# A hybrid decoder layer on Trainium2: three feature tiles of the GLU's input loaded and split during k, y reloaded in place of summed, DMA scratch set to 512 bytes

## The chip, the cores and the metric

The kernel runs on one core of one Trainium2 chip. The metric is the device time of one execution in microseconds (us); before the change it is 688.62 us, the median of 3 runs (688.46 to 688.71).

## The reference, cut to what matters

One layer: RMS norm, one wide projection, windowed attention beside a state space block with a GLU (gated linear unit), an output projection, and a gate from an embedding. 1024 tokens, width 1024, 8 heads of 64.

```python
z = rms_norm(h, mix_norm) @ w_in
q, k, v, gate_a, u, gate_s = jnp.split(z, splits, axis=-1)
attn = dilated_mixture_attention(q, k, v, q_norm, k_norm) * jax.nn.silu(gate_a)
...
yg = jax.nn.gelu(y, approximate=False)                    # y: the S5 scan's output, 512 features
ssm = yg * jax.nn.sigmoid(yg @ w_glu + b_glu) * jax.nn.silu(gate_s)
h = h + jnp.concatenate([attn, ssm], axis=-1) @ w_out
gate = jax.nn.sigmoid(rms_norm(h, ple_norm) @ w_ple_gate)
h = h + gate * (p @ w_ple_proj)
```

## The kernel before

Every float32 product is made of three fp32r matmuls (`mm3`, lines 106 to 109): each operand is split into a high part (a copy by ScalarE, ACT) and a low part (source minus high part, by VectorE, DVE, or GpSimd, POOL). Activations lie feature major, 128 features on the partitions and 512 tokens in a tile.

The stages follow each other: the u projection and the S5 scan (its gelu output goes to DRAM as `yg_s`, 4 feature tiles of 128 by 2 halves of 512 tokens); the gates (to `sg_s`, `sa_s`); q, then k, token major (lines 694 to 731); v (863 to 873); the GLU (877 to 921); the output projection of the state space half (`os`, 953), which is woven with attention; that of the attention half (`oa`, 974); the embedding gate. Attention is a generator (line 754): `step(n)` lets it advance by n heads. It makes scores into PSUM tiles `sc`, masks them and takes the row minimum on DVE (line 780, `p`), the exponential on ACT (803), splits them into two f16 halves `hl` (806 to 810), transposes these by a DMA into `pt` (812) and multiplies them with v into `pv` (818).

No order is written out by hand: the Tile framework places the instructions of each engine by a priority (`tc.high_priority`) and its own model of time, and each engine then runs its list in that order. Every DMA of this kernel is issued by SyncE (the queue SP), also the transposes `pt`; SP waits in order too.

The GLU before. Each of the 8 tiles `yl` (4 features by 2 token halves) is loaded into one of the four buffers `ev` (lines 897 to 899) and split into `ygh`, `ygl` (900), which lie in the pool `mp`. This pool is opened after `ph1.close()` (line 875), in the room of the x tiles that the v projection reads until its end. For each of 8 output tiles (n, f), 12 matmuls make `glu` in PSUM. Then:

```python
E[RY].tensor_tensor(y, yg[n][0][:, f].bitcast(F32), yg[n][1][:, f].bitcast(F32), op=OP.add)   # 915
nc.sync.dma_start(gl, sg_s[f * P:(f + 1) * P, c])                                              # 916
E[EG[f]].tensor_tensor(y, y, gl, op=OP.mult)                                                   # 917
A.activation(gl, o, AF.Tanh, bias=bg[:, f:f + 1], scale=0.5)                                   # 918
stt(y, gl, 1.0, y, OP.add, OP.mult)                                                            # 919
split(ms_[n][0][:, f], ms_[n][1][:, f], y, E[EM[f]])                                           # 920
```

Here `RY` is "V", so line 915 builds y again on DVE as the sum of its two parts; line 917 is on POOL, 918 on ACT, 919 and the split's low part on DVE. `y` (tile `ym`) and `gl` (tile `gm`) take two of the four `ev` buffers. In the trace line 919 appears as L281 and the splits as L736 (ACT) and L737 (DVE or POOL).

## Time and profile before

| | |
|---|---|
| median of 3 runs | 688.62 us (688.46 to 688.71) |
| the profiled execution: span from first to last instruction | 686.2 us |
| what lies around the span, taken from the median | 2.4 us |
| PE busy | 630.0 us, 92% |
| DVE busy | 496.8 us, 72% |
| POOL busy | 302.0 us, 44% |
| ACT busy | 289.5 us, 42% |
| bytes moved by DMA | 87.25 MB, mean 127 GB/s |

No time of its own is listed for the profiled execution; 688.6 us (its span and the 2.4 us around it) stands for it. PE is TensorE's matmuls, DVE VectorE, ACT ScalarE, POOL GpSimd. Busy shares over the whole span hide the stages: one has to ask for the busy time of each engine in a stretch, for what ended PE's idle time there, and for the clock that TensorE was granted. A DMA share is the mean busy share of 16 DMA engines, and can pass 1 where packets overlap.

### The profile page before, as it was taken

To read this page: it belongs to the slowest core of one execution; us is meant where nothing else is said; L and a number is where in the kernel's file an instruction comes from. 1 tells how busy PE (TensorE), PEld (TensorE's weight loads), DVE (VectorE), ACT (ScalarE), POOL (GpSimd) and SP (SyncE) were. 2 spreads that over 40 slices of the span, in tenths; PEclk is the share of its full clock that TensorE was granted. 3 is DMA by queue.
4 is the path that set the end of the run, shared out by engine and by line. 5 is a ranking of instruction groups with operands and counts; after the bars stand their busy time and mean duration, and the time that the engine had idled before them with its cause. 6 is when DMAs were issued, how large, how long until landed. Compare 5 with 4: busy or idle time off the path is not lost.

```text
span 686.2 us, 10942 instructions
## 1 busy us (share of the span) xinstructions
PE 630.0 (92%) x3836; PEld 491.9 (72%) x3836; DVE 496.8 (72%) x1126; ACT 289.5 (42%) x553; POOL 302.0 (44%) x230
## 2 busy tenths in 40 slices
PE   9997799777879999999899789889999999999997
PEld 6875577566768788877677556566677888888786
DVE  6999999899998557767553998957944766626322
ACT  7532123445576624348434646534513455113100
POOL 3433825866775224234332845422432437342641
PEclk9999899998999999999999889989999999999999
DMA  7803612323444746754661868899987243015101
GB/s 257 241 7 109 209 38 76 105 79 93 77 92 92 167 69 125 159 86 125 161 122 48 216 147 148 213 192 191 217 226 244 94 152 124 15 63 165 50 32 61
DMA packets 158119, 87.25 MB, mean 127 GB/s; under 512 B 117232, under 2 KB 130416, under 8 KB 158064
## 3 DMA queue, kind: packets, MB, share of 16 engines
q1 hardware_dynamic: 158064, 86.56, 50.7%
q8 instruction: 30, 0.49, 0.3%
q14 instruction: 25, 0.20, 0.1%
HBM read 48.81 MB, written 17.27 MB: 96 GB/s over the span
## 4 chain that ended last, share of the span: by engine, by line
PE 46%; DVE 26%; DMA 12%; issue 7%; ACT 5%; POOL 2%; SPq 1%; DVEq 0%; ACTq 0%; POOLq 0%
PE gt L108 4%; PE gt L109 4%; PE gt L107 3%; DMA wr<-in_w_in 3%; DMA pt<-hl 3%; PE oa L107 2%; PE oa L109 2%; PE oa L108 2%; DVE tmp L270 2%; PE q L109 2%; PE q L107 2%; PE q L108 2%; DVE wl L158 2%; DVE p L780 2%; PE k L108 2%
## 5 line engine op out<-in xcount | busy, mean ns | idle before, releaser
L158 POOL TENSOR_TENSOR wl<-wr,wh 128x512 fp32r<-128x512 f32 x34 | 49.4, 1457 | 67.8 <-ACT wh L157 44.5
L157 ACT ACTIVATE wh<-wr 128x512 fp32r<-128x512 f32 x68 | 41.9, 626 | 51.4 <-DMA wr<-in_w_in 22.4
L810 POOL TENSOR_TENSOR hl<-p,hl 128x384 f16<-128x384 f32 (+2 forms) x34 | 38.9, 1148 | 53.9 <-ACT hl L807 27.1
L107 PE MATMUL g<-xh,wh 128*128 128x512 f32 x128 | 52.6, 411 | 7.3 <-DVE gate L640 5.5
L109 PE MATMUL g<-xh,wl 128*128 128x512 f32 x128 | 52.5, 410 | 5.3 <-DVE wl L158 5.3
L803 ACT ACTIVATE p<-p,st 128x384 f32<-128x384 f32 (+4 forms) x64 | 39.8, 622 | 39.1 <-DVE st L780 38.9
L108 PE MATMUL g<-xl,wh 128*128 128x512 f32 x128 | 52.0, 407 | 0.0
L108 PE MATMUL gt<-hl,wh 128*128 128x512 f32 (+1 forms) x136 | 51.7, 381 | 0.0
L107 PE MATMUL gt<-hh,wh 128*128 128x512 f32 (+1 forms) x136 | 51.7, 382 | 0.0
L109 PE MATMUL gt<-hh,wl 128*128 128x512 f32 (+1 forms) x136 | 51.2, 382 | 0.0
L158 DVE TENSOR_TENSOR wl<-wr,wh 128x512 fp32r<-128x512 f32 x34 | 34.8, 1025 | 19.1 <-ACT wh L157 14.0
L1016 ACT ACTIVATE gg<-gg 128x512 f32<-128x512 f32 (+1 forms) x17 | 10.1, 605 | 67.4 <-DVE gg L270 67.2
L1018 POOL TENSOR_TENSOR gg<-gg,hs 128x512 f32<-128x512 f32 x14 | 18.0, 1290 | 43.1 <-DVE gg L270 41.5
L107 PEld LDWEIGHTS g<-xh,wh 128*128 128x128 f32 x128 | 24.6, 192 | 13.7 <-DVE gate L640 6.5
L270 DVE TENSOR_TENSOR gg<-gt,rrow 128x512 f32<-128x512 f32 (+1 forms) x17 | 10.8, 656 | 32.7 <-PE gt L109 32.6
L109 PEld LDWEIGHTS g<-xh,wl 128*128 128x128 f32 x128 | 24.7, 193 | 12.0 <-DVE wl L158 6.6
L818 PE MATMUL pv<-vv,pt 128*128 128x64 f16 x504 | 24.4, 198 | 6.3 <-DMA pt<-hl 6.2
L818 PEld LDWEIGHTS <-pt 128*128 128x128 f16 x504 | 19.0, 101 | 14.8 <-DMA pt<-hl 8.9
L107 PEld LDWEIGHTS gt<-hh,wh 128*128 128x128 f32 x136 | 25.6, 188 | 5.5
L108 PEld LDWEIGHTS gt<-hl,wh 128*128 128x128 f32 x136 | 25.6, 188 | 5.4
L109 PEld LDWEIGHTS gt<-hh,wl 128*128 128x128 f32 x136 | 25.6, 188 | 5.4
L780 DVE CUSTOM_DVE_ANT_0 p<-sc,mask,gc 128x128 f32<-128x128 f32 (+3 forms) x56 | 24.3, 458 | 6.7 <-PE sc L793 3.2
(330 smaller groups left out, 1957.2 us busy)
## 6 DMA issues: line engine op xcount, KB each, us to landing
wr<-in_w_in SPq DMA_DIRECT2D x48, 256.0 KB, 2.9
xr<-in_x SPq DMA_DIRECT2D x16, 256.0 KB, 4.7
wr<-in_w_out SPq DMA_DIRECT2D x16, 256.0 KB, 3.3
xos<-in_x SPq DMA_DIRECT2D x16, 256.0 KB, 4.0
h_s<-xos SPq DMA_DIRECT2D x16, 256.0 KB, 3.4
xoa<-h_s SPq DMA_DIRECT2D x16, 256.0 KB, 2.8
wr<-in_w_ple_gate SPq DMA_DIRECT2D x16, 256.0 KB, 3.0
out_t<-gg SPq DMA_DIRECT2D x15, 256.0 KB, 2.0
```

The lines of the kernel that those rows point to most:

```text
L107: T.matmul(o, lh, rh, start=first, stop=False)
L108: T.matmul(o, lh, rl, start=False, stop=False)
L109: T.matmul(o, ll, rh, start=False, stop=last)
L157: A.activation(hi, raw, AF.Copy)
L158: E[lo_on[k % len(lo_on)]].tensor_tensor(lo, raw, hi.bitcast(F32), op=OP.subtract)
L270: V.tensor_tensor(o, x, y, op=op)
L780: V.tensor_tensor_reduce(out, sc, msk, gm, init, op0=OP.add, op1=OP.min, accum_out=acc_[:, hd:hd + 1])
L803: A.activation(pb_, pb_, AF.Exp, bias=mx[:, hc], scale=-1.0, accum_out=dn[:, hc])
L810: E[LE[b][h0 % len(LE[b])]].tensor_tensor(hl[:, na:2 * na], pr_[:, 0:na], hl[:, 0:na], op=OP.subtract)
L818: T.matmul(pv[:, hd], pt[:, nf + i * nt + j + na * lp, :], vv[:, k0 + j, hd, lv, :], start=first, stop=end and not nf and j == n - 1 and l ...
L1016: A.activation(gt_, gt_, AF.Sigmoid)
L1018: (V if last else Q).tensor_tensor(gt_, gt_, hs, op=OP.add)
```

## The change

Four edits. (1) `RY` becomes "D": y of the GLU's gate is read again from `yg_s` by a DMA, in place of the sum on DVE. (2) Of token half 0, feature tiles 0, 1 and 2 are loaded and split inside the k loop, ahead of the row pairs 0, 1, 2, into two tiles of a new pool `y0p` that lies in room of its own. (3) In the GLU stage feature tile 3 of half 0 gets two tiles `yx` in `mp`; the two four-tile buffers `ygh0`, `ygl0` of `mp` are no longer taken. (4) `dynamic_dma_scratch_size` is set to 512 bytes per partition; the built program before reserves 16384 there. Comments are also cut.

```diff
-RY = "V"
+RY = "D"
...
+    y0p = ph2.enter_context(tc.tile_pool(name="y0p", bufs=1))
...
+    y0 = tuple(y0p.tile([P, 3, 512], F32R, name=f"yg{x}0") for x in "hl")
     for which, c0 in (("q", 0), ("k", 512)):
         w = [load_w(wp, a["w_in"], k, c0) for k in range(KT)]
         for bp in range(4):
+            if which == "k" and bp < 3:
+                y = ev(f"yl{bp}0")
+                nc.sync.dma_start(y, yg_s[bp * P:(bp + 1) * P, 0:512])
+                split(y0[0][:, bp], y0[1][:, bp], y, E[EY[bp]])
...
     for n in range(2):
-        yg.append((quad(f"ygh{n}"), quad(f"ygl{n}")))
+        if n:
+            yh_, yl_ = quad(f"ygh{n}"), quad(f"ygl{n}")
+            yg.append(tuple([t_[:, k] for k in range(4)] for t_ in (yh_, yl_)))
+        else:
+            yg.append(tuple([t_[:, k] for k in range(3)] + [mp.tile([P, 512], F32R, tag="yx", name=f"yx{j}", bufs=2)]
+                            for j, t_ in enumerate(y0)))
         for k in range(4):
+            if not n and k < 3:
+                continue
             y = ld(f"yl{k}{n}")
...
-    nc = bacc.Bacc("TRN2", target_bir_lowering=False, num_devices=1)
+    nc = bacc.Bacc("TRN2", target_bir_lowering=False, num_devices=1, dynamic_dma_scratch_size=512)
```

`EY = "QVQVQVQV"` puts the low parts of the tiles k = 0 and 2 of half 0 on POOL (Q) and that of k = 1 on DVE (V).

The framework places everything anew. Three places of its lists follow; names end in a running number that differs between the two programs, and lines of the change stand 6 to 13 higher from the k loop on (`split` is L697 in the change, L737 before; the mask's row minimum is L786, was L780).

**SP during k.** Here `qh`, `ql`, `ks` are the transposed q and k, `wr` the raw weights of v. Before:

```order
L725 DMA_TRANSPOSE qh_2296<-qh5_2631 128x8x128
L152 DMA wr2_1024_3138<-in_w_in 128x512
L726 DMA_TRANSPOSE ql_2297<-ql5_2632 128x8x128
L725 DMA_TRANSPOSE qh_2296<-qh6_2715 128x8x128
L726 DMA_TRANSPOSE ql_2297<-ql6_2716 128x8x128
L725 DMA_TRANSPOSE qh_2296<-qh7_2722 128x8x128
L726 DMA_TRANSPOSE ql_2297<-ql7_2723 128x8x128
L731 DMA_TRANSPOSE ks_2298<-k0_2854 128x8x128
L731 DMA_TRANSPOSE ks_2298<-k1_2859 128x8x128
```

With the change:

```order
L735 DMA_TRANSPOSE qh_2299<-qh5_2636 128x8x128
L152 DMA wr2_1024_3155<-in_w_in 128x512
L705 DMA yl00_2781<-yg_s_67 128x512
L736 DMA_TRANSPOSE ql_2300<-ql5_2637 128x8x128
L735 DMA_TRANSPOSE qh_2299<-qh6_2720 128x8x128
L736 DMA_TRANSPOSE ql_2300<-ql6_2721 128x8x128
L705 DMA yl10_2872<-yg_s_67 128x512
L735 DMA_TRANSPOSE qh_2299<-qh7_2727 128x8x128
L736 DMA_TRANSPOSE ql_2300<-ql7_2728 128x8x128
L741 DMA_TRANSPOSE ks_2301<-k0_2863 128x8x128
L705 DMA yl20_2963<-yg_s_67 128x512
L741 DMA_TRANSPOSE ks_2301<-k1_2868 128x8x128
```

The three loads stand between transposes that the k stage issues anyway.

**DVE at the start of the GLU.** `sc31` is block 3's scores of head 1, `p` their masked copy, `hl` its f16 halves. Before:

```order
L737 TENSOR_TENSOR ygl0_3712<-yl10_3717,ygh0_3711 128x512
L737 TENSOR_TENSOR ygl0_3712<-yl30_3725,ygh0_3711 128x512
L809 CAST hl26_3947<-p26_3941 128x384
L281 SCALAR_TENSOR_TENSOR vv_3124<-v7_3618,vscale_3125,vv_3124 128x8x64
L780 ISA p31_4190,st3_4148<-sc31_4191,mask_2313,gc_2305 128x512
L780 ISA st3_4148 128x1
L158 TENSOR_TENSOR wl3_0_3708<-wr3_0_3705,wh3_0_3707 128x512
L809 CAST hl23_3819<-p23_3813 128x384
L809 CAST hl24_3861<-p24_3855 128x384
L270 TENSOR_TENSOR ga0_4112<-at0_4114,ga0_4112 128x512
L737 TENSOR_TENSOR ygl1_3730<-yl11_3735,ygh1_3729 128x512
L915 TENSOR_TENSOR ym00_3762<-ygh0_3711,ygl0_3712 128x512
```

With the change:

```order
L697 TENSOR_TENSOR yx1_3729<-yl30_3730,yx0_3728 128x512
L697 TENSOR_TENSOR ygl1_3735<-yl11_3740,ygh1_3734 128x512
L815 CAST hl26_3952<-p26_3946 128x384
L786 ISA p31_4195,st3_4153<-sc31_4196,mask_2316,gc_2308 128x512
L786 ISA st3_4153 128x1
L281 SCALAR_TENSOR_TENSOR vv_3141<-v7_3635,vscale_3142,vv_3141 128x8x64
L270 TENSOR_TENSOR ga0_4117<-at0_4119,ga0_4117 128x512
L158 TENSOR_TENSOR wl3_0_3725<-wr3_0_3722,wh3_0_3724 128x512
L815 CAST hl23_3824<-p23_3818 128x384
L815 CAST hl24_3866<-p24_3860 128x384
L786 ISA p32_4218,st3_4153<-sc32_4219,mask_2316,gc_2308 128x512
L786 ISA st3_4153 128x1
```

The low part of tile 1 and the sum `ym00` are gone from this piece, half 1's first low part has moved up by nine places, and the next scores follow.

**SP in the middle of the GLU.** `pt` is an attention transpose, `gm` the gate load, `ym` the reload of y. Before:

```order
L812 DMA_TRANSPOSE pt30_4159<-hl30_4156 128x8x128
L916 DMA gm20_3847<-sg_s_65 128x512
L812 DMA_TRANSPOSE pt27_4101<-hl27_4098 128x6x128
L812 DMA_TRANSPOSE pt31_4199<-hl31_4196 128x8x128
L152 DMA wr4_512_4051<-in_w_out 128x512
L152 DMA wr5_512_4057<-in_w_out 128x512
L916 DMA gm30_3889<-sg_s_65 128x512
L812 DMA_TRANSPOSE pt32_4222<-hl32_4219 128x8x128
```

With the change:

```order
L926 DMA ym20_3851<-yg_s_67 128x512
L152 DMA wr4_512_4056<-in_w_out 128x512
L818 DMA_TRANSPOSE pt30_4164<-hl30_4161 128x8x128
L818 DMA_TRANSPOSE pt31_4204<-hl31_4201 128x8x128
L929 DMA gm20_3852<-sg_s_65 128x512
L818 DMA_TRANSPOSE pt32_4227<-hl32_4224 128x8x128
L926 DMA ym30_3893<-yg_s_67 128x512
L152 DMA wr5_512_4062<-in_w_out 128x512
L818 DMA_TRANSPOSE pt33_4267<-hl33_4264 128x8x128
L929 DMA gm30_3894<-sg_s_65 128x512
```

Each tile now has two loads that wait for an `ev` buffer, where it had one, and attention's transposes stand behind both.

## Rows read from the trace of the kernel before

**Rows 1.** The page: span, and busy time of each engine over it.

```profile
span 686.2 us, 10942 instructions
PE 630.0 (92%) x3836; PEld 491.9 (72%) x3836; DVE 496.8 (72%) x1126; ACT 289.5 (42%) x553; POOL 302.0 (44%) x230
```

**Rows 2.** Busy time by stretch: k, v's end, the GLU and a piece of it, attention.

```profile
core 0: us, PE busy (x) PEld busy (x) DVE busy (x) ACT busy (x) POOL busy (x), PEclk, DMA share, GB/s
280.00:300.00 20.00, 20.00 (x87) 16.10 (x86) 12.63 (x43) 7.28 (x12) 4.09 (x4) 1.00 0.69 117
360.00:370.00 10.00, 10.00 (x53) 7.96 (x49) 1.45 (x4) 2.62 (x5) 0.00 (x0) 1.00 0.01 2
374.20:445.00 70.80, 58.82 (x585) 40.52 (x586) 68.87 (x141) 41.72 (x91) 42.67 (x33) 0.88 0.77 176
...
400.00:410.00 10.00, 7.34 (x49) 5.03 (x49) 10.00 (x17) 4.78 (x11) 4.41 (x4) 0.66 0.71 165
445.00:521.00 76.00, 71.51 (x883) 50.95 (x871) 50.99 (x133) 28.95 (x62) 24.11 (x19) 0.96 0.98 210
```

**Rows 3.** PE's groups in 374.2 to 445: busy, mean ns, idle before, releasers.

```profile
L793 PE MATMUL sc<-ks,qh 128*128 128x256 f16 (+1 forms) x21 | 6.9, 344 | 4.3 <-DVE st L780 4.3
...
L750 PE MATMUL sc<-ks,qh 128*32 128x128 f16 x60 | 3.1, 228 | 4.0 <-DVE st L780 3.9
...
L818 PE MATMUL pv<-vv,pt 128*128 128x64 f16 x198 | 9.7, 203 | 1.8 <-DMA pt<-hl 1.8
```

**Rows 4.** DVE's group of the sum in 374.2 to 445, columns as in rows 3.

```profile
L915 DVE TENSOR_TENSOR ym<-ygh,ygl 128x512 f32<-128x512 f32 x8 | 10.0, 1248 | 0.0
```

**Rows 5.** Tiles ym and yl: duration ns minimum, median, maximum; first and last start.

```profile
L915 DVE TENSOR_TENSOR ym<-ygh,ygl x8: 678/1240/1782, 383.4 to 426.9; 128x512 f32<-128x512 f32 x8
...
L899 SPq DMA_DIRECT2D yl<-yg_s x8: 319/327/572, 326.6 to 378.5; - x8
L736 ACT ACTIVATE ygh<-yl x8: 613/631/638, 373.0 to 382.8; 128x512 fp32r<-128x512 f32 x8
L737 POOL TENSOR_TENSOR ygl<-yl,ygh x4: 1290/1293/1712, 373.7 to 384.2; 128x512 fp32r<-128x512 f32 x4
L737 DVE TENSOR_TENSOR ygl<-yl,ygh x4: 826/1262/1778, 375.5 to 385.3; 128x512 fp32r<-128x512 f32 x4
...
DMA to landing us min/median/max: 2.6/3.6/4.6
```

**Rows 6.** Timeline of PE: first and last matmul of two GLU tiles (start, us).

```profile
403.73 0.79 PE L107 MATMUL glu<-ygh,wh 128*128 128x512 f32 x1 [0.80 <-ACT gm L918]
...
408.58 0.63 PE L109 MATMUL glu<-ygh,wl 128*128 128x512 f32 x1
...
411.25 0.47 PE L107 MATMUL glu<-ygh,wh 128*128 128x512 f32 x1
...
413.89 0.40 PE L109 MATMUL glu<-ygh,wl 128*128 128x512 f32 x1
```

**Rows 7.** SP's waits in 374 to 460 at gate loads: us, times, longest.

```profile
SPq L916 <- DVE msl L737: 2.5, 2, 1.3
...
SPq L916 <- DVE ym L281: 1.9, 1, 1.9
...
SPq L916 <- DVE ygl L737: 1.4, 1, 1.4
...
SPq L916 <- DVE hl L809: 1.0, 1, 1.0
SPq L916 <- DVE st L780: 0.9, 1, 0.9
```

**Rows 8.** The page: DMA queues, packets, MB, share of 16 engines.

```profile
q1 hardware_dynamic: 158064, 86.56, 50.7%
q8 instruction: 30, 0.49, 0.3%
q14 instruction: 25, 0.20, 0.1%
```

More of the change, by code (lines that the diff above doesn't have):

```diff
@@ L692, in per_head, with split @@
         return x.unsqueeze(2).to_broadcast([P, 8, 64])
+    def split(hi, lo, src, eng=Q):
+        A.activation(hi, src, AF.Copy)
+        eng.tensor_tensor(lo, src, hi.bitcast(F32), op=OP.subtract)
+    y0 = tuple(y0p.tile([P, 3, 512], F32R, name=f"yg{x}0") for x in "hl")
     for which, c0 in (("q", 0), ("k", 512)):
@@ L733, in hybrid_layer @@
     ma, ms_ = {}, {}
-    def split(hi, lo, src, eng=Q):
-        A.activation(hi, src, AF.Copy)
-        eng.tensor_tensor(lo, src, hi.bitcast(F32), op=OP.subtract)
     def mdense(b, n):
@@ L899, in hybrid_layer @@
                 nc.sync.dma_start(y, yg_s[k * P:(k + 1) * P, n * 512:(n + 1) * 512])
-                split(yg[n][0][:, k], yg[n][1][:, k], y, E[EY[4 * n + k]])
+                split(yg[n][0][k], yg[n][1][k], y, E[EY[4 * n + k]])
     for n in range(2):
@@ L906, in hybrid_layer @@
             for k in range(4):
-                mm3(o, w[k][0][:, f * P:(f + 1) * P], w[k][1][:, f * P:(f + 1) * P], yg[n][0][:, k], yg[n][1][:, k],
+                mm3(o, w[k][0][:, f * P:(f + 1) * P], w[k][1][:, f * P:(f + 1) * P], yg[n][0][k], yg[n][1][k],
                     k == 0, k == 3)
@@ L914, in hybrid_layer @@
                 else:
-                    E[RY].tensor_tensor(y, yg[n][0][:, f].bitcast(F32), yg[n][1][:, f].bitcast(F32), op=OP.add)
+                    E[RY].tensor_tensor(y, yg[n][0][f].bitcast(F32), yg[n][1][f].bitcast(F32), op=OP.add)
                 nc.sync.dma_start(gl, sg_s[f * P:(f + 1) * P, c])
```

## The prediction

> **What bounds the kernel now.** I read the page's busy shares first: PE is busy 630.0 of 686.2 us [rows 1]. So at most 56 us of idle time are there to be won, and one must know in which stage they lie. Busy time by stretch is the second view [rows 2]. During k PE has no gap (20.00 of 20 us) and the others have room. At the end of v, from 360 to 370, DVE does 1.45 us of work in 10 and POOL none. Then, from 374.2 to 445, the roles turn: DVE is busy 68.87 of 70.8 us and PE only 58.82, at a mean granted clock of 0.88. This is the GLU stage, woven with attention, and it is the one that the change touches. From 445 to 521 PE is busy 71.51 of 76 and DVE 50.99: PE leads again.
>
> The third view is what ended PE's idle time in the GLU stage [rows 3]. The scores wait 4.3 and 3.9 us for the mask's row minimum on DVE (L780), pv only 1.8 us for a transpose. So DVE is what is waited for, not because L780 is long but because it queues in a full DVE. Of PE's 12.0 us idle (70.8 less 58.82) 8.2 are put down to DVE.
>
> The fourth is PE's timeline [rows 6]. After pauses the granted clock falls: it is 0.66 between 400 and 410 [rows 2], part of that stretch at 1.2 GHz and part at 2.4. A GLU tile of 12 matmuls took 5.48 us there (403.73 to 409.21), and 3.04 us from 411.25 on, at 2.4 GHz. A stall of PE thus costs more than its own length.
>
> **The sums that go from DVE.** Line 915 runs 8 times, 9.99 us in all (8 times 1248 ns [rows 4]). One DVE split of half 0, tile 1, leaves this stage too: 1.26 us at its median there [rows 5]. Together 11.25 us, the upper end. The same instructions in their shortest form took 678 and 826 ns [rows 5], which makes 6.25 us, the lower end: the sum's range of 678 to 1782 ns for one and the same shape says that more than the arithmetic is in it, and POOL is busy 42.67 of these 70.8 us [rows 2]. If the excess is waiting for POOL, another instruction may inherit it. I take the middle, 8.8 us, since POOL loses only two of its 33 instructions here, and most conflicts stay with the remaining splits.
>
> The Trainium skill says this outright (SBUF — State Buffer, section Who interferes with whom): a DVE instruction with two SBUF inputs contends with a GpSimd instruction that reads SBUF, and a DMA contends with no engine. By that rule the excess is time in a lock that passes to another instruction, the relief would be only the lower end, and the kernel would take 685.0 us; by the row alone it would be 680.0. The trace agrees as far as the spread of the durations goes; who inherits the wait no run here shows.
>
> Is a shorter DVE list worth its full length? DVE is full from 400 to 410 and nearly so over the stage [rows 2], and PE has 12 us of idle time to give back, more than the relief, so up to there neither PE nor the later part caps it; I pass it on one to one. The stretch from 445 on has PE busy 94%, so an earlier start moves it as a whole.
>
> **The loads that come.** Eight reloads `ym` are issued by SP at 327 ns each, by the row of `yl`, the same 256 KB of the same tensor [rows 5]: 2.6 us. SP works in order, and the lists show attention's transposes directly behind them. I charge all 2.6 us to the path; if SP has slack it is 0, the lower end. The `ym` load stands one to three transposes ahead of its `gm` load, so it lands before that, and line 917, which waits for both, is held no longer than by `gm`. As for bandwidth, 8 times 256 KB are 2.1 MB; the stage moves 176 GB/s at a share of 0.77 [rows 2], about 229 GB/s at full share, so the reloads add 9.2 us of all engines' time and lift the share to about 0.90. I take nothing for it, as the stretch behind runs at 0.98 with PE busy 94%; at most the 1.8 us that pv waits for transposes double.
>
> **The splits that move to k.** Three loads (1.0 us of SP), three ACT copies (1.9 us at 631 ns), two POOL subtractions (2.6 us at 1293 ns) and one on DVE (1.26 us at the median) [rows 5] now stand in k. Cover: between 280 and 300 ACT is busy 7.28 of 20 us, POOL 4.09, DVE 12.63, with PE never idle [rows 2]. I take 0. If the cover fails, it is because the three tiles take turns in the four `ev` buffers with the raw k tiles and hold up their evacuation; then ACT and DVE parts add up to 3.2 us.
>
> **What the early splits bring at the GLU's start.** Before, the first `ygh` copy starts at 373.0, as v ends, since its tile lies in v's room, and the last low part at 385.3 [rows 5]. Now tiles 0 to 2 are there, tile 3 and half 1 follow at once, so the elementwise chain starts some us earlier. This is no term of its own: while DVE is full, what starts earlier only fills DVE earlier.
>
> **The scratch.** All data moves on one queue of kind hardware_dynamic, and there are two for instructions [rows 8]; no queue of another kind is in the trace that would use the reserved room. Costs nothing; it makes room for the new tiles.
>
> **Sum.** Against the profiled execution (686.2 us and 2.4 around it, equal to the median by how I took it): 688.6 - 8.8 + 2.6 = **682.4 us**, 0.9% less. Its own ends: 688.6 - 11.25 = 677.4 with nothing paid on SP, and 688.6 - 6.25 + 2.6 + 1.8 = 686.8; 677.4 to 686.8 is this case's own range.
>
> **The rivals.**
>
> 1. *Deeper: DVE's relief also keeps the clock up.* All 11.25 us go, SP pays nothing, and the slow GLU tile between 403 and 409 runs as the next one did (5.48 - 3.04 = 2.4 us): 688.6 - 11.25 - 2.4 = 675.0 us. For it: the clock is under 1 in the very stretches where PE waits for DVE. Against: SP's new loads, and PE will still pause.
>
> 2. *Slower: SP's queue takes DVE's place.* A `ym` load cannot go out before its `ev` buffer is free, and SP holds everything behind it, transposes above all. Gate loads wait in just this way today: 2.5 us in two, 1.9, 1.4, 1.0 and 0.9 in one each [rows 7], a mean of 1.28 us over six. If each of the eight reloads stalls SP by that and its 327 ns, and attention feels it in full, 12.9 us come in and 8.8 go: 692.7 us. It decides from 8.8 / 8 = 1.1 us per reload, issue and stall, on. For it: both loads of a tile now wait for buffers which DVE and POOL free late. Against: six of the eight gate loads already wait so, and the second load of a tile finds a buffer of the same pair; a freer DVE frees buffers sooner; and transposes have some lead (pv lost 1.8 us in the stage). The Trainium skill (DMA: Bandwidth & Descriptors, section Anatomy of one DMA) states the rule behind this case: DMA engines wait for no semaphore, the issuing sequencer does so ahead of dispatch. The rows of SP's waits agree.
>
> 3. *Nothing: the stage is held by latency, not by DVE's load.* With four `ev` buffers only two output tiles are in flight; each goes through loads (2.6 to 4.6 us to land), POOL, ACT, DVE, ACT, DVE. If this loop sets the pace, DVE gets idle and the end stays: 688.6 us. For it: the loop has the same number of buffers as before. Against: the DVE is full now, so the loop isn't what waits.
>
> That the change doesn't do what it says can be set aside: the lists show neither L915 nor half 0's old splits in the GLU.
>
> **Chances.** About 0.2% (1.4 us) is what a measurement of this kernel can tell from no change. The forecast case gets 0.53, rival 1 0.13, rival 2 0.22, rival 3 0.12. Faster by over 0.2%: the first two, 0.66. Within 0.2%: 0.12. Slower by over 0.2%: 0.22. The predicted time is the forecast's, 682.4. The range starts at 676.0, leaving out the deep half of rival 1, and ends at 691.0, past the middle of rival 2 (1.4 us per reload, stall and issue, against 1.6 for its full price); outside lie some 0.06 and 0.10.
>
> **What would show it.** In the changed profile, DVE's busy time falls by 5 to 11 us over the span, with no line for the sum. If the forecast holds, the GLU stage shrinks by some 6 us, PE's waits for L780 (8.2 us) shrink by about half and the k stage keeps PE at 20 in 20. If rival 2 holds, SP's waits at the `ym` loads stand in the queue's view with over 1 us each, and pv's wait for `pt` rises well over 1.8 us. If rival 3 holds, DVE shows idle time before the tanh or line 917 while the stage keeps its length. If rival 1 holds, the granted clock between 380 and 440 is at 1.0 in most slices. I would be wrong altogether if the k stage gained PE gaps over 3 us, or if the framework's new order of attention left PE without work behind 445, where I counted on a plain shift.

## The result, and the profile after

The changed kernel takes **693.56 us** (median of 4 runs, 692.91 to 695.77) against 688.66 us for the kernel before on the same chip: ratio 1.0075, 95% interval 1.0051 to 1.0100. It is slower by 4.9 us, where 682.4 was forecast, and 2.6 us above the end of the range. (Run 2 below holds one execution of 847.46 us and run 5 one of 701.48 us that count as slow; the ratios leave them out, the medians do not.)

The profiled execution took 692.91 us, 691.1 of them in its span. The page, answering to [rows 1]:

```profile
span 691.1 us, 10937 instructions
...
PE 632.7 (92%) x3836; PEld 494.8 (72%) x3836; DVE 489.7 (71%) x1118; ACT 289.1 (42%) x553; POOL 304.8 (44%) x230
```

DVE does 7.1 us less than before, as intended. Where the time went is read stage by stage, from the first and last matmul of each kind of tile in the trace:

| stage | before | after | difference |
|---|---|---|---|
| start to first q matmul (same lists on every engine) | 222.1 | 224.3 | +2.2 |
| q, and k until the first v matmul | 95.0 | 95.4 | +0.4 |
| first v to first GLU matmul ("v stage") | 57.1 | 60.5 | +3.4 |
| first GLU to last `os` matmul ("GLU stretch", attention woven in) | 146.0 | 139.7 | -6.3 |
| last `os` to first `oa` matmul ("gap") | 0.3 | 1.9 | +1.6 |
| first to last `oa` matmul | 50.7 | 53.8 | +3.1 |
| embedding gate, to the last `gt` matmul | 109.9 | 110.4 | +0.5 |

In this execution the gain stands just where it was forecast, and in its size (a second execution, run 5, shows 4.3 us of it); it is lost ahead of it and behind it. Busy time by stretch, each stretch moved by 6 us (k by 2) against those of [rows 2]:

```profile
core 0: us, PE busy (x) PEld busy (x) DVE busy (x) ACT busy (x) POOL busy (x), PEclk, DMA share, GB/s
282.00:302.00 20.00, 20.00 (x87) 16.10 (x86) 10.18 (x34) 6.63 (x11) 5.33 (x5) 1.00 0.56 118
...
380.20:451.00 70.80, 60.36 (x666) 41.82 (x665) 65.51 (x155) 45.02 (x102) 43.26 (x33) 0.90 0.98 210
...
451.00:527.00 76.00, 70.49 (x805) 51.34 (x804) 47.10 (x111) 24.66 (x50) 24.59 (x17) 1.00 0.91 206
```

In the GLU stage DVE has room again (65.51 of 70.8 us, it was 68.87), PE is busier, and the DMA engines go from a share of 0.77 to 0.98. PE's groups there, answering to [rows 3]:

```profile
L824 PE MATMUL pv<-vv,pt 128*128 128x64 f16 x216 | 10.1, 196 | 7.7 <-DMA pt<-hl 7.6
L799 PE MATMUL sc<-ks,qh 128*128 128x256 f16 (+2 forms) x25 | 8.0, 342 | 2.1 <-DVE st L786 2.1
...
L756 PE MATMUL sc<-ks,qh 128*32 128x128 f16 x68 | 3.9, 226 | 0.2 <-DVE st L786 0.2
```

The waits for the row minimum on DVE fell from 8.2 to 2.3 us; the waits for transposes rose from 1.8 to 7.6. What DVE gave, the transposes took back in part. The reloads alone do not explain that: from 374 to 525 PE waits 5.6 us for transposes before, 11.0 with the change, and also 10.6 with the early splits alone (run 3) and 7.8 with neither sum nor reload (run 11).

**Ahead of it: k's side chain.** PE has no gap in k, but the work beside it falls behind. ScalarE's timeline in k: start, us, engine, line, operation, and in brackets the idle time before it with what ended it:

```profile
279.51 1.06 ACT L733 ACTIVATE qh<-rawq 128x1024 f16<-128x1024 f32 x1 [0.46 <-DMA qh<-qh]
286.02 0.63 ACT L696 ACTIVATE ygh<-yl 128x512 fp32r<-128x512 f32 x1 [5.45 <-DMA yl<-yg_s]
286.56 0.58 ACT L714 ACTIVATE sqk<-k 128x512 f32<-128x512 f32 x1
...
296.81 0.63 ACT L696 ACTIVATE ygh<-yl 128x512 fp32r<-128x512 f32 x1 [2.32 <-DMA yl<-yg_s]
...
306.98 0.63 ACT L696 ACTIVATE ygh<-yl 128x512 fp32r<-128x512 f32 x1 [3.18 <-DMA yl<-yg_s]
```

ScalarE runs its list in order; it stands three times, 10.9 us in all, before the copy of an early tile that has not landed, with the evacuation of k (`sqk`, L714, and `rawk`, L718) behind it. Not all of this is new idle time: before, ScalarE stood there 5.9 us for a raw q tile from POOL and 4.8 until a transpose had landed, and from 268 to 318 its busy time only falls from 25.4 to 22.9 us. What counts is that the work on k comes later. The casts of k, last start in the row, end that chain. Before and after, by tile:

```profile
L729 ACT ACTIVATE k<-rawk x8: 614/631/632, 294.7 to 327.7; 128x512 f16<-128x512 f32 x8
```

```profile
L739 ACT ACTIVATE k<-rawk x8: 614/629/652, 300.7 to 333.9; 128x512 f16<-128x512 f32 x8
```

The last one starts 10.6 us behind the first v matmul (317.1) before, 14.2 behind it (319.7) after. v's evacuations and attention's first heads are in the same lists, and PE pays in v: it waits longer for `vv` on DVE. PE's waits from 314 to 382, before and after (us, times, longest):

```profile
PE v L107 <- DVE vv L281: 1.3, 1, 1.3
```

```profile
PE v L107 <- DVE vv L281: 2.9, 1, 2.9
```

The v stage has the same 324 matmuls in both. PE's idle time in it goes from 2.9 to 4.5 us and its busy time from 54.2 to 56.0, at a mean granted clock of 0.97 for 1.00: the clock fell behind this wait (last section). With the early splits alone (run 3) the clock stays at 1.00, and the idle time is 5.5 us.

**Behind it: the last weights of `oa`.** The half of `w_out` that `oa` needs is loaded second (the runs' texts call it the second half), through two raw tiles, and its four last tiles can be cast only when the last `os` matmuls have read the tiles in their place. SyncE's and then ScalarE's, DVE's and PE's timelines after, around the last `os` matmul (519.92):

```profile
515.84 0.39 SPq L766 DMA_DIRECT2D ga<-sa_s  x1
...
517.84 0.46 SPq L964 DMA_DIRECT2D h_s<-xos  x1
520.96 2.25 SPq L948 DMA_DIRECT2D xoa<-h_s  x2
523.31 0.38 SPq L964 DMA_DIRECT2D h_s<-xos  x1
524.88 0.81 SPq L152 DMA_DIRECT2D wr<-in_w_out  x2
```

```profile
521.11 0.63 ACT L696 ACTIVATE mah<-ga 128x512 fp32r<-128x512 f32 x1 [5.67 <-DVE ga L270]
521.68 1.28 ACT L157 ACTIVATE wh<-wr 128x512 fp32r<-128x512 f32 x2
529.63 1.30 ACT L157 ACTIVATE wh<-wr 128x512 fp32r<-128x512 f32 x2 [6.67 <-DMA wr<-in_w_out]
```

```profile
530.96 1.19 DVE L158 TENSOR_TENSOR wl<-wr,wh 128x512 fp32r<-128x512 f32 x1 [5.40 <-ACT wh L157]
...
532.68 0.68 DVE L281 SCALAR_TENSOR_TENSOR xoa<-oa,xoa 128x512 f32<-128x512 f32 x1
```

```profile
530.03 0.40 PE L109 MATMUL oa<-mah,wl 128*128 128x512 f32 x1
533.41 0.51 PE L107 MATMUL oa<-mah,wh 128*128 128x512 f32 x1 [2.99 <-DVE xoa L281]
```

Read backwards: PE stands 2.99 us because both PSUM tiles of `oa` are full; the one due is emptied by DVE, in whose list the weights' low part stands first; that waits for ScalarE's cast, the cast for a load, and the load went out at 524.88, behind loads of `xoa` and spills on SyncE. SyncE's own waits from 490 to 535, before and after:

```profile
SPq L935 <- DMA h_s<-xos: 10.2, 7, 2.5
```

```profile
SPq L948 <- DMA h_s<-xos: 18.2, 8, 5.1
```

A buffer of `ev` comes free when the spill from it has landed, and until then the next load into it holds SyncE's whole list. Attention now ends at 503.4 instead of 509.7, so more `os` tiles follow each other through these buffers undiluted; that this is why SyncE waits longer is not shown. Run 3 speaks against it as the whole reason: there attention ends at 519.9, SyncE's waits for spills are 10.6 us, much as before the change, and `oa` loses more. What the losing kernels share is when the last two weights' loads go out. SyncE's timeline before and in run 3, where the last `os` matmul starts at 520.22 and 522.64:

```profile
520.76 0.85 SPq L152 DMA_DIRECT2D wr<-in_w_out  x2
```

```profile
527.86 2.23 SPq L152 DMA_DIRECT2D wr<-in_w_out  x2
```

They go out 0.5 us behind the last `os` matmul before, 5.0 us behind it with the change and 5.2 us in run 3.

### The profile page after: what moved, and what is told of

It is laid out like the page before. It is cut to its first block, busy times and chain, and to the rows that moved or that the text cites. A ratio compares the mean times of both kernels' runs of the same rounds, so it can differ in the third digit from the quotient of the medians.

```text
span 691.1 us, 10937 instructions
## 1 busy us (share of the span) xinstructions
PE 632.7 (92%) x3836; PEld 494.8 (72%) x3836; DVE 489.7 (71%) x1118; ACT 289.1 (42%) x553; POOL 304.8 (44%) x230
## 4 chain that ended last, share of the span: by engine, by line
PE 38%; DVE 24%; DMA 16%; issue 8%; ACT 6%; POOL 5%; SPq 2%; POOLq 0%; ACTq 0%; DVEq 0%
DMA pt<-hl 4%; DMA wr<-in_w_in 4%; PE gt L108 4%; PE gt L109 4%; PE gt L107 4%; DVE tmp L270 2%; PE oa L107 2%; PE oa L108 2%; PE oa L109 2%; DVE wl L158 2%; DVE y L578 2%; DVE tmp L275 1%; DVE p L786 1%; PE g L108 1%; POOL wl L158 1%
## 5 line engine op out<-in xcount | busy, mean ns | idle before, releaser
L158 POOL TENSOR_TENSOR wl<-wr,wh 128x512 fp32r<-128x512 f32 x34 | 50.9, 1500 | 62.8 <-ACT wh L157 60.2
L816 POOL TENSOR_TENSOR hl<-p,hl 128x384 f16<-128x384 f32 (+2 forms) x34 | 41.9, 1232 | 59.0 <-ACT hl L813 31.8
L157 ACT ACTIVATE wh<-wr 128x512 fp32r<-128x512 f32 x68 | 41.9, 626 | 46.0 <-DMA wr<-in_w_in 25.4
L107 PE MATMUL g<-xh,wh 128*128 128x512 f32 x128 | 54.3, 424 | 5.4 <-DVE gate L640 5.4
L109 PE MATMUL g<-xh,wl 128*128 128x512 f32 x128 | 53.8, 421 | 4.2 <-DVE wl L158 4.1
L108 PE MATMUL gt<-hl,wh 128*128 128x512 f32 (+1 forms) x136 | 51.7, 381 | 0.0
L109 PE MATMUL gt<-hh,wl 128*128 128x512 f32 (+1 forms) x136 | 51.2, 382 | 0.0
L158 DVE TENSOR_TENSOR wl<-wr,wh 128x512 fp32r<-128x512 f32 x34 | 31.9, 937 | 19.1 <-ACT wh L157 19.1
L815 DVE CAST hl<-p 128x384 f16<-128x384 f32 (+2 forms) x34 | 21.1, 624 | 19.9 <-DMA pt<-hl 14.2
L109 PEld LDWEIGHTS g<-xh,wl 128*128 128x128 f32 x128 | 25.4, 198 | 11.6 <-DVE wl L158 5.8
L107 PE MATMUL oa<-mah,wh 128*128 128x512 f32 x64 | 25.5, 399 | 4.5 <-DVE xoa L281 3.0
L108 PEld LDWEIGHTS g<-xl,wh 128*128 128x128 f32 x128 | 25.6, 200 | 5.6 <-issue 0.2
```

What stands on the lines that cost most here:

```text
L107: T.matmul(o, lh, rh, start=first, stop=False)
L108: T.matmul(o, lh, rl, start=False, stop=False)
L109: T.matmul(o, ll, rh, start=False, stop=last)
L157: A.activation(hi, raw, AF.Copy)
L158: E[lo_on[k % len(lo_on)]].tensor_tensor(lo, raw, hi.bitcast(F32), op=OP.subtract)
L815: V.tensor_copy(hl[:, 0:na], pr_[:, 0:na])
```

## The experiments

Each run is timed beside the kernel before, 689.3 to 689.75 us there; single executions of one kernel spread over 4 to 10 us, so ratios and intervals carry the verdicts. Stages in us are from one profiled execution each: the two of the changed kernel differ by 2.0 us in the GLU stretch, the traces of runs 10, 11, 12 and 15 are of their fastest execution, and that of run 8 is of its slowest; "cast lag" is from the last `os` matmul to the start of the last `w_out` cast on ScalarE.

| kernel | v stage | GLU stretch | gap + oa | cast lag | ratio to before (95%) |
|---|---|---|---|---|---|
| before | 57.1 | 146.0 | 51.0 | 5.6 | 1 |
| changed, first | 60.5 | 139.7 | 55.7 | 10.4 | 1.0075 (1.0051 to 1.0100) |
| changed, again | 60.3 | 141.7 | 54.7 | 9.6 | 1.0056 (1.0033 to 1.0079) |
| 1 scratch alone | 57.2 | 145.2 | 51.2 | 5.7 | 1.0003 (0.9986 to 1.0019) |
| 2 reload alone | 55.9 | 142.3 | 58.4 | 10.5 | 1.0034 (1.0010 to 1.0057) |
| 3 early splits alone | 60.3 | 143.7 | 58.8 | 10.8 | 1.0131 (1.0108 to 1.0154) |
| 4 changed, early loads ahead of q | 57.8 | 142.5 | 54.3 | 9.3 | 0.9983 (0.9962 to 1.0005) |
| 6 changed, weights on ScalarE's queue | 60.2 | 141.6 | 50.9 | 5.6 | 1.0005 (0.9979 to 1.0032) |
| 7 reload, six residual tiles | 56.2 | 142.6 | 55.0 | 8.2 | 1.0001 (0.9982 to 1.0020) |
| 8 runs 4 and 6 together | 58.3 | 145.1 | 51.0 | 6.1 | 0.9992 (0.9971 to 1.0012) |
| 9 reload, weights on ScalarE's queue | 57.3 | 145.6 | 51.1 | 5.9 | 0.9997 (0.9978 to 1.0016) |
| 10 before, weights on ScalarE's queue | 56.6 | 146.3 | 51.6 | 6.2 | 1.0050 (1.0026 to 1.0073) |
| 11 no sum, no reload | 56.8 | 138.8 | 55.2 | 8.4 | 0.9986 (0.9969 to 1.0003) |
| 12 sum twice | 56.8 | 153.9 | 52.7 | 7.6 | 1.0176 (1.0147 to 1.0205) |
| 13 run 11, weights on ScalarE's queue | 57.5 | 144.4 | 51.7 | 6.3 | 0.9951 (0.9928 to 0.9975) |
| 14 reload, four raw tiles | 57.6 | 144.7 | 54.4 | 0.2 | 1.0056 (1.0038 to 1.0075) |
| 15 reload, four raw and six residual tiles | 57.7 | 145.0 | 50.7 | 0.2 | 1.0057 (1.0036 to 1.0078) |
| 16 run 15 with the sum | 57.4 | 145.6 | 50.8 | 0.5 | 1.0011 (0.9986 to 1.0036) |

q and k together, which the table leaves out, take 94.9 to 95.9 us in all kernels but three: with six residual tiles (runs 7, 15, 16) they take 98.6 to 98.8. PE there has two waits at the start of q that no other kernel has, here in run 15:

```profile
PE q L107 <- DVE gate L640: 2.4, 1, 2.4
...
PE q L107 <- ACT wh L157: 0.7, 1, 0.7
```

So these tiles have a price of their own, up to 3 us ahead of the stages in the table, and the times of the three runs contain it.

In all eighteen traces but run 14's, gap and `oa` go by the moment of the last two loads of `w_out`: 50.7 to 51.7 us where the first of them goes out at most 1.2 us behind the last `os` matmul, 52.7 to 58.8 where it goes out 3.1 us or more behind it. Run 14 loses time in `oa` with these loads early, at another wait (see there).

**1. The scratch alone.** Before, with

```diff
-    nc = bacc.Bacc("TRN2", target_bir_lowering=False, num_devices=1)
+    nc = bacc.Bacc("TRN2", target_bir_lowering=False, num_devices=1, dynamic_dma_scratch_size=512)
```

> Kernel before with the DMA scratch set to 512 and nothing else; no instruction changes its place. Theory A: the 2.2 us by which the changed kernel is behind when q begins (first q matmul at 224.3 instead of 222.1 us), in a stretch where the instructions are the same, is chance of one execution: time within 0.2% of before, 687.3 to 690.0 us, and the first q matmul within 0.7 us of 222.1. Rival B: the scratch, or the addresses that move with it, costs the 2.2 us: 690.3 to 691.5 us, first q matmul at about 224.

689.53 us against 689.55: no effect, A in time. The first q matmul came at 223.8, outside A's window, in a kernel that is not slower; the changed kernel's second execution had it at 222.9. So the 2.2 us ahead of q are the spread of executions, and the first profile overstates the stages' loss by them.

**2 and 3. The reload alone, and the early splits alone.** The kernel before with the first edit, the changed kernel with the second:

```diff
-RY = "V"
+RY = "D"
```

```diff
-RY = "D"
+RY = "V"
```

> Kernel before with y reloaded from DRAM for the gate in place of summed on VectorE, and nothing else. Theory A: the 6.3 us that the GLU stretch (first GLU matmul to last os matmul, 146.0 before, 139.7 after) gains come from the sum that VectorE no longer does, and the loss around oa (1.6 us before it begins, 3.1 us in it) comes with the gain, since os tiles are left over behind attention: GLU stretch 139 to 142 us, oa loses 2 to 5 us, time 684.5 to 688.5. Rival B: the loss around oa comes from the early splits and not from the reload: 681.5 to 683.5. Rival C: the stretch gains only because GLU's first input lies ready, not by the missing sum: 688 to 690, GLU stretch 145 or more.

> The changed kernel with y summed on VectorE again: the early loads and splits and the scratch stay. Theory A: the early splits make the stage of v longer (60.5 us after, 57.1 before, from the first v matmul to the first GLU matmul) and VectorE's sum takes the gain of the GLU stretch away: v stage 60 to 61 us, time 691 to 695. Rival B: the early splits cost nothing and what the changed kernel loses, it loses behind attention through the reload: v stage 57 to 58 us, time 687.5 to 690.

691.8 and 698.45 us. The reload shortens the GLU stretch by 3.7 us, and gap and `oa` lose 7.4, more than A allowed: the time fell out of A's range, B and C fell altogether. The early splits make the v stage 3.2 us longer, as A said, but the time lies above A's range: what A had not foreseen is that gap and `oa` lose 7.8 with them too. The stretch gets 2.3 us shorter with the splits alone. Apart the two parts cost 0.34% and 1.31%, together 0.56 to 0.75%: they do not add up, and each loses in the same place behind attention.

**4. The early loads ahead of q.** The changed kernel with

```diff
+    for f in range(3):
+        nc.sync.dma_start(y0[1][:, f].bitcast(F32), yg_s[f * P:(f + 1) * P, 0:512])
     for which, c0 in (("q", 0), ("k", 512)):
...
-                y = ev(f"yl{bp}0")
-                nc.sync.dma_start(y, yg_s[bp * P:(bp + 1) * P, 0:512])
-                split(y0[0][:, bp], y0[1][:, bp], y, E[EY[bp]])
+                split(y0[0][:, bp], y0[1][:, bp], y0[1][:, bp].bitcast(F32), E[EY[bp]])
```

> The changed kernel with the three feature tiles loaded ahead of q, straight into the tiles that will hold their low parts, and split in place during k: no tile of the four-buffer set is taken and no split waits for a transfer; the same ScalarE, VectorE and GpSimd instructions stand in k. Theory A: k's side chain falls behind because ScalarE, in order, stands at the splits' loads (idle 5.45, 2.32 and 3.18 us there) with k's evacuations behind it: the last k cast ends some 11 us behind the first v matmul as before (after: 14.5), the v stage takes 57 to 58 us, time 689.0 to 691.0. Rival B: it is the splits' own work on ScalarE, VectorE and GpSimd: the last k cast stays 14 us or more behind the first v matmul, the v stage stays at 60 us or more, time 692.5 to 694.5.

The v stage falls to 57.8, the time to 689.08 (ratio 0.9983). The casts of k:

```profile
L739 ACT ACTIVATE k<-rawk x8: 615/628/632, 295.2 to 328.8; 128x512 f16<-128x512 f32 x8
```

The last starts 11.0 us behind the first v matmul (317.8). The same ACT, DVE and POOL instructions stand in k, so their work is worth 0.7 us of v at most, and the wait for the loads and the shared buffers 2.5 to 2.7. A is shown. The ratio falls by 0.73%, 5 us, against run 5, more than v's share; where the rest goes is not shown.

**5. The changed kernel again.**

> The changed kernel unaltered, on one chip with the three that follow, since single executions of one kernel here spread over some 4 us. Theory A: the loss is as large as first seen (ratio 1.0075) and all of it lies behind the start of k: ratio 1.005 to 1.010, v stage 60 to 61 us, first q matmul anywhere from 221 to 225 us. Rival B: the 2.2 us by which its first profiled execution was behind at q was a part of the measured loss and is chance: ratio 1.002 to 1.005.

693.71 us, ratio 1.0056; A's stages, though the interval reaches into B. Stages now differ from before by 0.8, 0.2, 3.2, -4.3, 1.5, 2.2 and 0.5: again a gain in the middle and a larger loss around it.

**6. The last weights from another queue.** `load_w` gets a queue, ScalarE's for the second half of `w_out`, in the changed kernel:

```diff
-        nc.sync.dma_start(raw, src[k * P:(k + 1) * P, c0:c0 + 512])
+        q.dma_start(raw, src[k * P:(k + 1) * P, c0:c0 + 512])
...
-... lo=LO[part], pri=LP[part])
+... lo=LO[part], pri=LP[part], q=A if part == "a" else None)
```

> The changed kernel with the eight loads of the second half of w_out issued on ScalarE's queue in place of SyncE's. Theory A: oa waits for its last weights because their loads stand on SyncE behind loads of h_s that wait for a spill to land (5.1 us at most): the last cast of w_out begins at 526 to 528 us in place of 530.3, oa takes 51 to 52 us in place of 53.8, ratio to the changed kernel 0.995 to 0.998. Rival B: those loads wait for the two raw tiles, which come free only when the last os matmuls have read the weights' own tiles: oa stays at 53.5 us or more and the time within 0.2% of the changed kernel.

688.37 us, ratio 1.0005 where the same changed kernel on the same chip had 1.0056. ScalarE's timeline, its own DMA issue as ACTq, and busy time from 510 to 550, where the changed kernel had PE busy 35.09 of 40 us:

```profile
519.32 0.91 ACTq L152 DMA_DIRECT2D wr<-in_w_out  x2
522.50 0.64 ACT L157 ACTIVATE wh<-wr 128x512 fp32r<-128x512 f32 x1 [3.88 <-DMA wr<-in_w_out]
524.81 0.63 ACT L157 ACTIVATE wh<-wr 128x512 fp32r<-128x512 f32 x1 [1.67 <-DMA wr<-in_w_out]
```

```profile
510.00:550.00 40.00, 39.97 (x175) 32.13 (x174) 22.97 (x29) 15.41 (x27) 12.90 (x10) 1.00 0.56 178
```

The last loads go out 5.6 us earlier (519.32, not 524.88), `oa` has no wait left and takes 50.7. SyncE still stands 17.4 us for spills from 490 to 535, but no weights stand behind them. A is shown, and goes a little beyond its numbers (the last cast at 524.8, forecast for 526 to 528): SyncE's list cost gap and `oa` 3.8 us.

**7. Six residual tiles of their own.** The reload and the scratch, with

```diff
-                xr = ev(f"xo{part}{f}{n}")
+                xr = rp.tile([P, 512], F32, tag="xo", name=f"xo{part}{f}{n}", bufs=6)
```

> The kernel before with the reload of y and the scratch at 512, and the tiles of the output projection's residual in six buffers of their own in place of the four that they share. With four, the reload alone took 2.0 us from the last os matmul to the first oa matmul and 56.4 us in oa, against 0.3 and 50.7 before. Theory A: the os tiles left over behind attention turn in four buffers, each held until its spill has landed, and that holds up SyncE's list with the last weights on it: gap and oa together 51 to 54 us, time 685.5 to 688 where before is at 688.7 to 689.6. Rival B: the weights' own tiles and the two raw tiles hold up oa: gap and oa stay at 56 us or more, time 689.5 to 692.

689.86 us; gap and `oa` 55.0, between A and B. Half the loss goes: SyncE still waits 12.8 us for spills from 508 to 536 and the weights are still 8.2 us late. The time contains some 3.7 us by which q and k are longer here.

**8 to 10. The repairs combined, without the early splits, and alone.** Run 6's edit on run 4, on run 2 and on the kernel before.

> Both repairs on the changed kernel: the three feature tiles loaded ahead of q and split in place (ratio to before 0.998 alone), and w_out's second half loaded from ScalarE's queue. Theory A: the two losses are separate and both go: v stage 57 to 58 us, oa 51 to 52 us, ratio to before 0.994 to 0.997. Rival B: the second repair does nothing: ratio 0.997 to 1.000, oa at 52.9 us or more.

> The kernel before with the reload of y, no early splits, and w_out's second half loaded from ScalarE's queue. Theory A: the reload alone was worth 4.9 us up to the last os matmul (v stage 55.9 for 57.1, GLU stretch 142.3 for 146.0) and lost 7.4 in the gap and in oa; with the weights off SyncE's list the loss goes (gap 0.3, oa 50.7) and the gain stays: ratio to before 0.991 to 0.996, some 683 to 686.5 us. Rival B: the loads on ScalarE cost in the GLU stretch what they save behind it, as in the kernel with both repairs (GLU stretch 145.1): ratio 0.997 to 1.002.

> The kernel before with w_out's second half loaded from ScalarE's queue and nothing else. In the kernel before oa has no wait to lose (gap 0.3, oa 50.7 us). Theory A: the repair only takes away a wait that the reload and the early splits had made: ratio 0.998 to 1.002, oa 50.7. Rival B: the move is worth something by itself in the GLU stretch (SyncE's list gets shorter): ratio below 0.997; rival C: ScalarE pays for the issues: ratio above 1.003.

688.66, 689.29 and 691.72 us. In all three `oa` is whole (50.7, 50.8, 51.4), as A said, but with the weights' loads moved the GLU stretch is 145.1 and 145.6, so that the gain is gone there. That is rival B for run 9; run 8 has A's `oa` and B's ratio. Run 10's ratio is rival C's; its profiled execution, the fastest of seven (688.7), does not show where its time goes.

**11 and 12. Without the sum, and with it twice.** The kernel before with

```diff
-                    E[RY].tensor_tensor(y, yg[n][0][:, f].bitcast(F32), yg[n][1][:, f].bitcast(F32), op=OP.add)
+                    pass
...
-                E[EG[f]].tensor_tensor(y, y, gl, op=OP.mult)
+                E[EG[f]].tensor_tensor(y, yg[n][0][:, f].bitcast(F32), gl, op=OP.mult)
```

and, in run 12, the kernel before with

```diff
                     E[RY].tensor_tensor(y, yg[n][0][:, f].bitcast(F32), yg[n][1][:, f].bitcast(F32), op=OP.add)
+                    E[RY].tensor_tensor(y, yg[n][0][:, f].bitcast(F32), yg[n][1][:, f].bitcast(F32), op=OP.add)
```

> The kernel before with the eight sums taken out and nothing in their place: the gate multiplies the high part of y alone, the low part is left out of it. VectorE is relieved as by the reload, without the eight loads. GLU stretch, gap and oa together took 197.0 us before (146.0, 0.3, 50.7) and 200.7 with the reload alone. Theory A: VectorE's sum is on the path there and the reload's transfers give the gain back: 188 to 192 us, ratio to before 0.988 to 0.994. Rival B: the sum is beside the path; scores, casts, transposes and pv decide, and freeing VectorE only turns waits for its minima (9.2 us) into waits for transposes (6.2 us): 196 to 198 us, ratio 0.998 to 1.002.

> The kernel before with each of the eight sums done twice, one after the other: the cost doubled, some 10 us more of VectorE. Theory A (the sum is on the path): GLU stretch, gap and oa 201 to 207 us in place of 197.0, ratio 1.006 to 1.015. Rival B (beside the path): 196.5 to 199 us, ratio 0.999 to 1.003.

688.15 and 701.64 us. DVE's rows of the two sums, and PE's waits from 340 to 530, with the sum twice:

```profile
L915 DVE TENSOR_TENSOR ym<-ygh,ygl 128x512 f32<-128x512 f32 x8 | 9.5, 1191 | 0.0
...
L916 DVE TENSOR_TENSOR ym<-ygh,ygl 128x512 f32<-128x512 f32 x8 | 7.5, 933 | 0.0
```

```profile
PE sc L793 <- DVE st L780: 9.1, 7, 3.4
...
PE sc L750 <- DVE st L780: 3.2, 3, 1.5
```

PE's waits for the minima are 12.3 us, 9.2 in the same window before. Some 7 us more of DVE lengthen the stretch by 7.9 us and the traced execution's span by 10.2; by the medians the kernel is 11.9 us longer. The sum is on the path, A, with a ratio above A's top. Taken out, it shortens the stretch by 7.2 us, but `oa` gives back 4.2. The traced execution (684.77 us) is the fastest of twelve; by the ratio 0.14% is left, which cannot be told from nothing, and gap and `oa` with the stretch are 194.0 us, between A and B. VectorE's work counts in its stretch, at 0.7 to 1.1 us for each us of it; the end gets at most a part of what is taken out.

**13 and 14. No sum with ScalarE's loads; the reload with four raw tiles.** Run 11 with run 6's edit; the reload and the scratch with

```diff
-RAW = (3, 2)
+RAW = (3, 4)
```

> The kernel before without the eight sums (the gate multiplies the high part of y alone, the low part is left out of it) and with w_out's second half loaded from ScalarE's queue. Without the sums alone the GLU stretch took 138.8 us for 146.0, but oa 54.9 for 50.7. Theory A: what is gained up to the last os matmul is taken back by oa only through the late weights: with them off SyncE's list oa takes 50.7 and the stretch stays near 139, ratio to before 0.987 to 0.993. Rival B: the order that goes with ScalarE's loads costs the stretch what oa gains, whatever relieved VectorE (as it did with the reload, 145.6 for 142.3): stretch 142 or more, ratio 0.996 to 1.001.

> The kernel before with the reload of y, the scratch at 512 and four raw weight tiles behind attention's start in place of two, so that w_out's loads can land ahead of the jam on SyncE's list; nothing moves to another queue. With two raw tiles the reload alone had a GLU stretch of 142.3, a gap of 2.0 and 56.4 us in oa, ratio 1.0034. Theory A: oa's weights then wait for no load behind the last os matmul: gap and oa 51 to 53 us, stretch 141 to 144, ratio to before 0.991 to 0.997. Rival B: oa's weights wait for the tiles that the last os matmuls read, whatever is prefetched: gap and oa 55 us or more, ratio 1.000 to 1.004.

686.85 us (0.9951) and 693.32 us. Run 13 lies between its rivals: `oa` 51.5, but a stretch of 144.4. Run 14 fits neither rival: gap and `oa` are 54.4 us, and the ratio is above both. The weights are there 0.2 us behind `os`, and another wait has their place, on DVE, for the residual that SyncE loads late:

```profile
533.59 0.69 DVE L281 SCALAR_TENSOR_TENSOR xoa<-oa,xoa 128x512 f32<-128x512 f32 x1 [4.46 <-DMA xoa<-h_s]
```

So the cause is not the weights as such but SyncE's list behind unlanded spills (13.9 us of such waits from 508 to 536 in run 14), which holds either.

**15 and 16. Four raw and six residual tiles, with the reload and with the sum.** The edits of runs 7 and 14 together, with `RY = "D"` and with `RY = "V"`.

> The kernel before with the reload of y, the scratch at 512, four raw weight tiles and six residual tiles of their own together. Apart, the six tiles left the weights late (last cast 8.2 us behind the last os matmul, oa 54.8) and the four raw tiles left the residual late (one wait of 4.46 us on VectorE for h_s, oa 54.2). Theory A: oa's loss is these two waits, both from SyncE's list behind spills of h_s that have not landed: gap and oa together 51 to 52 us, and with a GLU stretch of 142 to 145 a ratio to before of 0.991 to 0.998. Rival B: with both out of the way a third wait comes (the clock, the transposes): gap and oa 53.5 us or more, ratio 0.999 to 1.005.

> The kernel just named with the sum on VectorE in place of the reload: the control for it. Theory A: the kernel before has no wait in oa to repair, so more tiles bring nothing: gap and oa 51 us, ratio 0.998 to 1.003, and the reload is worth 3 to 5 us between the two. Rival B: the tiles alone shorten the stretch, and the reload adds nothing to them: ratio equal to that of the kernel with the reload, within 0.2%.

Gap and `oa` are 50.7 and 50.8 us: with both waits gone `oa` loses nothing, A for that. But the times are 692.48 and 691.15 us (1.0057 and 1.0011). The reload is worth less than nothing here (neither A nor B of run 16 allowed for that), and both stretches are 145 us. A part of the loss is the six tiles' own, the longer q and k; run 15's profiled execution (688.5) is again the fastest of seven and does not show the rest.

**What stays open.** In every kernel whose `oa` is repaired the stretch is 144.4 us or more, with the reload or without, save in run 6 (141.6). Why the earlier loads of weights take the stretch's gain was not settled: moving them also changes the order of attention's casts on ScalarE. And the reload's worth has no fixed sign: it costs 0.34% alone, wins 0.56 to 0.75% with the early splits (1.0131 to 1.0075 or 1.0056) and 0.53% with ScalarE's loads (1.0050 to 0.9997), and costs 0.46% with more tiles (1.0011 to 1.0057). No kernel run here that keeps both parts of y beats the kernel before by more than its interval; the nearest is run 4, 0.9983 (0.9962 to 1.0005).

## Why the prediction was wrong

**The sums that go (8.8, between 6.25 and 11.25): right in the stretch.** The eight sums without the split are 5.4 us of it at their shortest and 10.0 in full; without them the stretch is 7.2 us shorter (run 11). By the rule on shared ports that was weighed there (the Trainium skill, SBUF — State Buffer, section Who interferes with whom) the excess of the long sums would pass to other instructions, and only the 5.4 would be won. The runs lie between: 7.2 in the stretch, and the second of two sums (933 ns) is shorter than the first (1191 ns). They do not decide it.

**The loads that come (2.6): right in size, not in way.** The stretch is 142.3 with reloads and 138.8 with neither: 3.5 us, from single executions. But SyncE hardly stood at them, from 340 to 530 in the changed kernel:

```profile
SPq L926 <- DVE st L786: 3.2, 4, 1.7
...
SPq L926 <- DVE ygl L697: 1.2, 1, 1.2
...
SPq L926 <- DVE ym L281: 0.6, 1, 0.6
...
SPq L926 <- POOL ygl L697: 0.3, 1, 0.3
```

That is 5.3 us over seven waits, but the waits at the gate loads fell from 7.7 us [rows 7] to 2.0: SyncE stands at the two loads of a tile no longer than it stood at one. Its issue of a reload took 428 ns at the median, for 327. What rose is PE's wait for transposes, to 7.6 us, where at most a doubling of 1.8 was allowed.

**The net of the two (-6.2): its match in the first execution is in part luck.** The reload alone brings 3.7 us of stretch, where sums and loads without the split come to some 5; the early splits alone bring 2.3, where the text gave them about 1, the one DVE split, and "no term of its own" for the earlier start. The second execution has 4.3.

**The splits that move to k, at 0: the first step that failed.** The cover was read as busy time: ACT 7.28 of 20 us, PE without a gap. It held for the work (0.7 us at most, run 4) and failed for order: a list stands at a load that has not landed, with the k chain behind it. The text named the cause, tiles that take turns in `ev` with the raw k tiles, and an upper end of 3.2 us, which the range did not take in; 3.2 to 3.4 came, in v and not in k. The like numbers are luck, since the 3.2 was added up from work. The sign to look for, PE gaps in k of over 3 us, was thus the wrong one: k's PE stayed at 20 in 20.

**"An earlier start moves it as a whole": the second step that failed.** The stretch behind 445 was taken as a plain shift since PE is busy 94% there. But at its end stands a chain that does not shift: the weights' tiles come free with the last `os` matmul, and the last loads go out in SyncE's order, 5.0 us behind it in place of 0.5. Gap and `oa` lost 4.7 and 3.7 us in the two executions. The warning at the end ("left PE without work behind 445") is what happened, though the waits shown are for weights and not for attention.

**The rivals.** Rival 2 had the right mechanism, SyncE's list held by a load whose buffer is not free, at the wrong place: not at `ym`, but at `xos` and `xoa` behind spills of `h_s`, with the weights queued behind. The rule it was weighed with (the Trainium skill, DMA: Bandwidth & Descriptors, section Anatomy of one DMA), that the issuing sequencer does the waiting, fits the trace: SyncE waits 18.2 us for spills from 490 to 535. Rival 3 fell, since DVE's load does set the stretch (run 12). Rival 1's clock did not carry: the mean granted clock of the GLU stage went from 0.88 to 0.90 only.

**In sum,** by the second execution: -4.3 in the stretch for the forecast -6.2, then +3.4 in k and v for 0, +3.7 in gap and `oa` for 0, and 1.3 at the ends: 4.1 us, for a measured 0.56%, 3.9 us.

## What to carry to other kernels

A step moved under a busy engine is hidden only if no in-order list comes to stand at it: look up what its first instruction waits for, and what stands behind it in that list, before busy shares. A gain in one stretch reaches the end only if the next stage's first inputs do not hang on the last work of this one; follow the weights, residuals and buffers of the stage behind. And a change that makes a scheduler place everything anew should be timed together with its neighbours: here the same edit was worth from -0.7% to +0.5%, by what else was in the lists.

## What the runs showed of the hardware

Pauses of PE of the same length ended differently. In the changed kernel the granted clock stayed at 1.00 (2.4 GHz) behind the 2.99 us before 533.41; with the reload alone, behind 3.04 us at the same place in `oa`, it fell to 0.50 (1.2 GHz) until past 534, and matmuls came every 0.43 us in place of 0.23. The changed kernel, then the reload alone, columns as in the first windows above:

```profile
532.00:534.00 2.00, 0.59 (x3) 0.49 (x4) 1.36 (x3) 0.61 (x1) 0.00 (x0) 1.00 0.36 132
534.00:536.00 2.00, 2.00 (x10) 1.65 (x9) 1.29 (x2) 1.24 (x3) 0.46 (x1) 1.00 0.69 172
```

```profile
528.00:530.00 2.00, 0.56 (x1) 0.50 (x2) 1.38 (x3) 0.58 (x1) 0.00 (x0) 0.58 0.64 196
530.00:532.00 2.00, 2.00 (x6) 1.58 (x5) 1.29 (x2) 1.24 (x3) 0.43 (x1) 0.50 0.70 194
```

Thirteen matmuls at 0.2 us more are 2.6 us, the difference between that `oa` (56.4) and the changed kernel's (53.8). In the v stage of the changed kernel PE paused 2.87 us, worked again from 342.68 on at 1.00, and only then, at 344, fell to 0.50 until 347.4, with no new pause:

```profile
342.00:344.00 2.00, 1.32 (x6) 1.13 (x7) 2.00 (x7) 1.02 (x4) 1.00 (x1) 1.00 0.76 148
344.00:346.00 2.00, 2.00 (x7) 1.50 (x6) 2.00 (x7) 1.95 (x7) 0.56 (x2) 0.51 0.51 110
```

That doubled sums cost more than their own length goes with the clock too: its mean was 0.949 to 0.958 in the six executions with them, 0.957 to 0.973 in those of the kernel before beside them. The first q matmul, behind lists that are the same in the kernel before, the changed one and run 1, came at 222.1, 224.3, 222.9 and 223.8 us: two microseconds in a stage of one profiled execution are no effect.
